# Order edges for side work: squares, row scalings and their transfers behind the weight split of their k-step

## The chip, the cores and the metric

The kernel runs on one core of one Trainium2 chip. The metric is the device time of one execution in microseconds. A core has five engines with a queue of their own each: PE (matmul), DVE (vector), ACT (scalar), POOL (GpSimd) and SP, which in this kernel issues nearly all transfers. Each queue is worked off in order. Which instruction stands where in a queue is settled at compile time, by a scheduler that goes by the order in the program, by what it takes to be ready, and by order edges that the program adds.

## The reference

One layer of a hybrid encoder, applied to two groups of requests with shared weights, 1024 and 256 tokens wide (10 blocks of 128 tokens), and to 2 x 256 rows of memory. The kernel works the 10 blocks in two groups of 5 (640 rows each). Cut to what matters:

```
hn   = rms_norm(x, norm_g)                    # x: 1280 x 2048
proj = hn @ w_in                              # conv input, gates, dt, q, k, v, mq
mk, mv = split(rms_norm(mem, mem_norm_g) @ w_mem_kv)
o = concat(ssd(silu(conv(xbc)), dt) * silu(z), window_attention(q, k, v), mem_attention(mq, mk, mv))
y = x + o @ w_out
```

All is float32. rms_norm needs, for each row, the sum of its 2048 squares.

## The kernel before

**Matrix products.** Each product runs in k-steps of 128 features. In a k-step a weight tile (`wraw`) is loaded, then split into a high part `wh` (ACT, line 203) and the rest `wl` (DVE, line 204), and three matmuls use them: high by high, high by low, low by high. There are two kinds of block:
- `block_tok` (line 231): 5 token blocks (4 for the memory), 512 or 288 columns, 16 k-steps, matmuls in lines 256 to 258. The last two k-steps are worked together.
- `block_pair` (line 1116): a scheme with 7 in place of 8 products, 8 k-steps a unit, each with 21 matmuls of 320 columns (lines 1141 to 1143). POOL forms sums of the weights (`weight_sums`, line 1096, four instructions in line 1113), and these are split too (`sh`, `sl`, by the same lines 203 and 204). It yields after every k-step but k = 6, so 7 times a unit.

**The order of the work.** First the memory's two blocks and q (group 0); then `pairs_in(0)`, ten units; then the token blocks kv and mq of group 0; then `pairs_in(1)`, ten units for group 1; then token blocks with the two "lanes" beside them (attention, state space, memory attention: generators that `pump` moves on by rates); then the output blocks. In this profile the first pair stage runs from 166 to 426.6 us, the second from 525.6 to 772.8 us.

**Side work.** Beside a pair stage a generator `side` is moved on by one step at chosen k-steps (lines 1507 and 1508).
- `first_side` (line 1351), beside the first pair stage: the squares of x's row blocks 5 to 9, by `stats` (line 1319). A row block is 4 pieces of 128 x 512, each loaded into a tile `sst` (line 1341) and squared with a sum on ACT (line 1332); after the fourth come a sum on DVE (line 1335) and `rsqrt` on POOL (lines 121 and 122) into `rx`. `x_rows(1)` then spreads `rx` over the partitions by matmuls into `prx` (line 1407), copied to `rbc` (line 1408). Then 16 rows `xrow` of 128 x 640 are loaded (line 1358), scaled on DVE (line 1172) and stored to `xs_d` (line 1364), from where the second group's rows are loaded in the kv and mq blocks (line 1166).
- `next_side` (line 1367), beside the second pair stage: the squares of the memory's 4 row blocks, in the same way. Their `rx` is used much later, in the lanes.
- `sst` and `xrow` share one buffer (`tag="sq"`).
- `keep_x` (line 1411) stores the split x to memory, 16 transfers of 640 KB, called in every k-step from the second unit on.

**Order edges.** `wsplit` leaves its two instructions in `marks`. A block `with tc.issue_after(ins)` puts what it traces on the engine of `ins` behind `ins` in that engine's queue; it makes no engine wait for another. Before the change, the lanes' steps (line 142), the planned steps (lines 1227 and 1247) and the scaling of a row (line 1360) are put behind `marks`. The squares and the loads of rows are not; the squares' loads are put behind the last `fill_direct` load (line 1340).

Of the kernel before, what the change touches and what calls it, by code (L numbers as in the profile page):

```python
# [10 lines left out]
F32 = mybir.dt.float32  # L11
# [8 lines left out]
P = 128  # L20
D = 2048
# [20 lines left out]
def hymba_encoder_kernel(  # L42
# [77 lines left out]
    def rsqrt(dst, src, scale, n):  # L120
        G.tensor_scalar(out=dst, in0=src, scalar1=scale, scalar2=EPS, op0=ALU.mult, op1=ALU.add)
        G.tensor_tensor(out=dst, in0=dst, in1=mhalf[:, :n], op=ALU.pow)
# [59 lines left out]
    def fill_direct(q, j, src, gain=None, n=640, norm=False):  # L182
# [15 lines left out]
            V.scalar_tensor_tensor(out=l, in0=ch, scalar=gain, in1=h.bitcast(F32), op0=ALU.mult, op1=ALU.subtract)  # L198
        yield

    def wsplit(raw, h, l):

        a = A.activation(h, raw, AF.Copy)  # L203
        b = V.tensor_sub(l, raw, h.bitcast(F32))  # L204
        marks[:] = a.ins, b.ins
# [12 lines left out]
    def w_in_rows(name):  # L218
        return w_laid(laid_in(name), W_AT[name][1])
# [4 lines left out]
    def w_out_rows(c):  # L224
        return w_laid(w_out_laid[c], 512)
# [5 lines left out]
    def block_tok(w, nt, evac, before_last=None, feats=range(KT), places=range(KT)):  # L231

        load, n = w
        last = len(feats) - 1
        ps = [acc.tile([P, 512], F32, tag="acc", name="acc") for _ in range(nt)]
        hls = {}
        for k in range(last + 1):
            raw = wp.tile([P, 512], F32, tag="wraw", name="wraw", bufs=RB)
            load(feats[k], raw[:, :n])
            with tc.high_priority(offset=HP[2]):  # L240
                h = wp.tile([P, 512], F32R, tag="wh", name="wh", bufs=WB)
                l = wp.tile([P, 512], F32R, tag="wl", name="wl", bufs=WB)
                wsplit(raw[:, :n], h[:, :n], l[:, :n])
            hls[k] = h, l
            if k == last - 1:
                continue
            if k == last and before_last is not None:
                before_last(k)

            for t in range(nt):  # L250
                for k_ in ((k - 1, k) if k == last else (k,)):
                    q, m = divmod(places[k_], 4)
                    h, l = hls[k_]
                    sh = cur["H", q][:, m, t * P:(t + 1) * P]
                    sl = cur["L", q][:, m, t * P:(t + 1) * P]
                    T.matmul(ps[t][:, :n], sh, h[:, :n], start=(k_ == 0), stop=False)  # L256
                    T.matmul(ps[t][:, :n], sh, l[:, :n], start=False, stop=False)  # L257
# [910 lines left out]
    def x_row(grp, r):  # L1168
        return x_turned[grp, r * P:(r + 1) * P, :]

    def scale_row(r, x):
        V.scalar_tensor_tensor(out=x, in0=x, scalar=vec[:, R_G + r:R_G + r + 1], in1=rbc, op0=ALU.mult, op1=ALU.mult)

    def p_rows(k, tiles, new=True):

# [143 lines left out]
    def stats(tiles, place, ahead=4, group=None):  # L1319

        n = 4 * len(tiles)
        group = group or n
        pieces, s4 = {}, None
        for g in range(0, n, group):
            m = min(group, n - g)
            for i in range(m + ahead):
                if i >= ahead:
                    t, c = divmod(g + i - ahead, 4)
                    if c == 0:
                        s4 = sm.tile([P, 4], F32, tag="s4", name="xs4", bufs=4)  # L1330
                    x = pieces.pop(g + i - ahead)
                    A.activation(x, x, AF.Square, accum_out=s4[:, c:c + 1])
# [15 lines left out]
    def square_place(_):  # L1348
        return fin.tile([P, 640], F32, tag="sq", name="sst")[:, :512]

    def first_side():

        yield from stats([(xrow(t), t) for t in range(5, 10)], square_place, ahead=1)
        for _ in x_rows(1):
            yield
        for r in range(KT):
            x = fin.tile([P, 640], F32, tag="sq", name="xrow")
            S.dma_start(x, x_row(1, r))
            yield
            with ExitStack() as st:  # L1360
                for ins in marks:
                    st.enter_context(tc.issue_after(ins))
                scale_row(r, x)
                S.dma_start(xs_d[r], x)
            yield

    def next_side():
        yield from stats([(mrow(i), 10 + i) for i in range(4)], square_place, ahead=1)

    def run(gen, rates, after=None, hold=0, lag=2, extra=None):  # L1370

        for k in gen:
            if after is not None and k % 4 == 3:
                pend.extend(after(k // 4))
            if hold > 0:
                for _ in range(2 if k < KT - 4 else 0):
                    if pend:
                        u = pend.popleft()()
                        next(u)
                        next(u)  # L1380
# [12 lines left out]
            if extra is not None:  # L1393
                extra(k)
# [108 lines left out]
    def pairs_in(grp, extra, side):  # L1503
        nonlocal owe
        for u, unit in enumerate(units):
            for k in block_pair(w_in_pairs, u, rows_in, ev_seven(*unit, grp), lead=2):
                if grp == 0 and (u > 3 or k not in (3, 7)) or grp and k in (0, 2, 4):
                    next(side, None)

                owe = owe + (1.4 if k < 7 else 0.0) if left else 0.0  # L1510
                while owe >= 1:
                    owe -= 1
                    if left:
                        some_left()
                if u == 0:
                    extra(32 + k)
                elif grp == 0 and keep:
                    keep_x(*keep.pop(0))

    side = first_side()  # L1520
    pairs_in(0, p_step, side)
    assert next(side, None) is None

    def left_and(f):
        def g(k):
# [7 lines left out]
        extra=left_and(lambda k: t_step(16 + k)))  # L1533
    side = next_side()
    pairs_in(1, t_step, side)
    assert next(side, None) is None
    early.close()


# [22 lines left out]
    dtb, aneg = lconst([P, 32], "dtb"), lconst([P, 32], "aneg")  # L1562

    def tok(name, i, evac, after=None, extra=None, hold=0):
        run(block_tok(w_in_rows(name), 5, evac), RATES[name], after, extra=extra, hold=hold)

    queue(1, vectors, [0])
    queue(1, dt_prep, [0])
# [53 lines left out]
    halves = [range(8), range(8, KT)]  # L1622
    for c, part_ in ((0, 0), (1, 0), (0, 1), (1, 1)):
        h = halves[part_]
        run(block_tok(w_out_rows(c), 5, ev_out(c, part_), feats=h, places=h), RATES["o" if part_ else "oa"], hold=-1,
            extra=late_rows(c, part_))
    for c in (2, 3):
        j0 = 16 * c - 48
        for k in block_tok(w_out_rows(c), 5, ev_out(c), before_last=lambda _: beside_step(j0 + 14)):
# [90 lines left out]
```

## Time and profile before

| what | value |
|---|---|
| median of 3 runs | 1840.42 us (1840.4 to 1844.22) |
| the profiled execution's own time | 1843.13 us |
| its span, first to last instruction | 1841.4 us |
| mean granted clock of TensorE | 0.992 |
| DMA | 334.20 MB, 181 GB/s over the span |

A row of a group gives line, engine, operation, tiles (out<-in), shapes and count, then busy us and the mean ns of one, then the idle time of the engine just before these instructions and what ended most of it. A row of the timeline gives start, duration, engine, line, operation and tiles, and in brackets the idle time before it and its releaser. A row of the waits gives who waited for whom, the total in us, how often, and the longest. Line numbers are those of the kernel before. PE's busy share counts overlapping matmuls once; a matmul of 320 columns can show 0.3 us and yet start every 0.15 us.

### The profile page before, as it was taken

The numbers are of one execution on the slowest core, as the hardware profiler recorded it, in microseconds if no ns is written. First come the engines' busy times: TensorE is split into PE (matmuls) and PEld (weight loads), VectorE is DVE, ScalarE is ACT, GpSimd is POOL, SyncE is SP. The second block draws the span as 40 slices with busy tenths as digits, with TensorE's granted clock in tenths as the row PEclk, the third lists the DMA queues.
The fourth block names the chain that finished last, engine by engine and source line by source line (L and its number), as shares of the span: only waits on it lengthen the run. The fifth ranks groups of instructions, "written<-read, shape, count | busy, mean of one in ns | idle before, by whom it ended". The sixth has DMA issues, their size and how long they took to land.

```text
span 1841.4 us, 31026 instructions
## 1 busy us (share of the span) xinstructions
PE 1787.4 (97%) x10306; PEld 1577.7 (86%) x10306; DVE 1327.5 (72%) x2473; ACT 951.4 (52%) x2081; POOL 676.7 (37%) x1092
## 2 busy tenths in 40 slices
PE   9999999998999999999999999999999999999999
PEld 7777999988889999988777877888777787889999
DVE  4495788895767889787677767667797765766665
ACT  6554444344554444366567447657546744443332
POOL 0104788871057889511001011000111101047775
PEclk9999999999999999999999999999999999999999
DMA  8687335555753333374545567657698765644442
GB/s 285 208 301 275 121 108 183 179 176 168 257 166 108 116 115 102 102 218 140 164 139 154 171 219 257 211 177 225 210 283 242 252 201 158 208 152 147 144 133 86
DMA packets 216177, 334.20 MB, mean 181 GB/s; under 512 B 22160, under 2 KB 84944, under 8 KB 216016
## 3 DMA queue, kind: packets, MB, share of 16 engines
q1 hardware_dynamic: 215872, 332.16, 58.0%
q8 instruction: 81, 1.33, 0.3%
q14 instruction: 80, 0.66, 0.1%
q10 hardware_dynamic: 144, 0.06, 0.0%
HBM read 255.53 MB, written 76.61 MB: 180 GB/s over the span
## 4 chain that ended last, share of the span: by engine, by line
PE 67%; DMA 13%; DVE 8%; issue 4%; ACT 3%; POOL 3%; SPq 1%; ACTq 0%; DVEq 0%; POOLq 0%
PE acc L257 8%; PE acc L258 8%; PE acc L256 8%; PE acc L1143 8%; PE acc L1141 8%; PE acc L1142 8%; PE accm L1141 3%; PE accm L1142 3%; PE accm L1143 3%; DVE wl L204 2%; PE py L873 2%; DMA sst<-in_x_sample_dram 1%; POOL ws L1113 1%; DMA wraw<-in_w_in_pairs_dram 1%; DMA rf<-ac 1%
## 5 line engine op out<-in xcount | busy, mean ns | idle before, releaser
L256 PE MATMUL acc<-wh,xH 128*128 128x512 f32 (+1 forms) x1248 | 486.9, 390 | 9.4 <-ACT wh L203 7.6
L257 PE MATMUL acc<-wl,xH 128*128 128x512 f32 (+1 forms) x1248 | 481.8, 386 | 8.0 <-DVE wl L204 7.5
L258 PE MATMUL acc<-wh,xL 128*128 128x512 f32 (+1 forms) x1248 | 478.4, 383 | 0.0
L204 DVE TENSOR_TENSOR wl<-wraw,wh 128x512 fp32r<-128x512 f32 (+1 forms) x480 | 349.5, 731 | 162.9 <-ACT wh L203 160.1
L203 ACT ACTIVATE wh<-wraw 128x512 fp32r<-128x512 f32 (+1 forms) x480 | 290.4, 612 | 186.6 <-PE acc L258 103.7
L256 PEld LDWEIGHTS acc<-wh,xH 128*128 128x128 f32 x1248 | 237.7, 191 | 56.1 <-ACT wh L203 11.5
L257 PEld LDWEIGHTS acc<-wl,xH 128*128 128x128 f32 x1248 | 237.6, 190 | 55.9 <-DVE wl L204 15.1
L203 ACT ACTIVATE sh<-ws 128x384 fp32r<-128x384 f32 x224 | 115.8, 524 | 321.4 <-POOL ws L1113 148.9
L258 PEld LDWEIGHTS acc<-wh,xL 128*128 128x128 f32 x1248 | 237.6, 190 | 42.1 <-issue 0.7
L204 DVE TENSOR_TENSOR sl<-ws,sh 128x384 fp32r<-128x384 f32 x224 | 155.8, 698 | 126.4 <-ACT sh L203 125.9
L1113 POOL TENSOR_TENSOR ws<-wraw 128x128 f32<-128x128 f32 x224 | 148.3, 662 | 261.6 <-DMA wraw<-in_w_in_pairs_dram 111.5
L1113 POOL TENSOR_TENSOR ws<-wraw,ws 128x128 f32<-128x128 f32 x224 | 154.9, 691 | 17.5
L1113 POOL TENSOR_TENSOR ws<-ws,wraw 128x128 f32<-128x128 f32 x224 | 148.7, 664 | 0.0
L1113 POOL TENSOR_TENSOR wraw<-wraw 128x128 f32<-128x128 f32 x224 | 138.6, 619 | 17.6
L581 POOL COPY lg<-nsink 128x2 f32<-128x2 f32 x40 | 16.1, 405 | 269.9 <-PE ppt L609 146.9
L1143 PE MATMUL acc<-xH,wl 128*128 128x320 f32 x320 | 99.6, 311 | 4.9 <-DVE wl L204 4.9
L1141 PE MATMUL acc<-tH,sh 128*128 128x320 f32 x320 | 100.1, 313 | 0.0
L1141 PE MATMUL acc<-xH,wh 128*128 128x320 f32 x320 | 99.1, 310 | 0.7 <-ACT wh L203 0.6
L1143 PE MATMUL acc<-tH,sl 128*128 128x320 f32 x320 | 99.5, 311 | 0.0
L1141 PE MATMUL accm<-tH,wh 128*128 128x320 f32 x320 | 98.9, 309 | 0.2
L1142 PE MATMUL acc<-xL,wh 128*128 128x320 f32 x320 | 98.9, 309 | 0.0
L1142 PE MATMUL acc<-tL,sh 128*128 128x320 f32 x320 | 98.7, 308 | 0.0
(472 smaller groups left out, 3921.6 us busy)
## 6 DMA issues: line engine op xcount, KB each, us to landing
wraw<-in_w_in_pairs_dram SPq DMA_DIRECT2D x160, 256.0 KB, 2.7
wraw<-in_w_in_laid_dram SPq DMA_DIRECT2D x128, 256.0 KB, 3.6
wraw<-in_w_out_laid_dram SPq DMA_DIRECT2D x64, 256.0 KB, 3.4
wraw<-in_w_out_pairs_dram SPq DMA_DIRECT2D x64, 256.0 KB, 2.8
xH<-xH SPq DMA_DIRECT2D x16, 640.0 KB, 5.9
xL<-xL SPq DMA_DIRECT2D x16, 640.0 KB, 6.3
rf<-ac SPq DMA_DIRECT2D x40, 256.0 KB, 4.0
rb<-ac SPq DMA_DIRECT2D x40, 256.0 KB, 4.4
```

Of the source, the lines that this page charges most:

```text
L203: a = A.activation(h, raw, AF.Copy)
L204: b = V.tensor_sub(l, raw, h.bitcast(F32))
L256: T.matmul(ps[t][:, :n], sh, h[:, :n], start=(k_ == 0), stop=False)
L257: T.matmul(ps[t][:, :n], sh, l[:, :n], start=False, stop=False)
L258: T.matmul(ps[t][:, :n], sl, h[:, :n], start=False, stop=(k_ == last))
L581: G.tensor_copy(lg[:, :, nk:nk + 1], ns8[:, rr, :].unsqueeze(2))
L873: T.matmul(py[:, h * 64:h * 64 + 64], mt[:, (h % 4) * P:(h % 4 + 1) * P], xsT[g][:, h * 64:h * 64 + 64], start=True, stop=True)
L1113: G.tensor_tensor(out=o, in0=x, in1=y, op=op)
L1141: T.matmul(ps[p], h, xh, start=(k_ == 0), stop=False)
L1142: T.matmul(ps[p], h, xl, start=False, stop=False)
L1143: T.matmul(ps[p], l, xh, start=False, stop=(k_ == 7))
```

## The change

- `behind()` is a block that enters `issue_after` for each of the marks. `side_work(tasks)` runs a list of tasks (load, f), two loads ahead: in step i it first calls f of task i - 2 and then the load of task i, all in a `behind()` block.
- The squares become tasks: 7 pieces of 320 columns a row block (the last of 128), two buffers of 320 columns in place of one of 640, 35 tasks beside the first pair stage and 28 beside the second. Their loads are no longer put behind the last `fill_direct` load.
- The scalings become 32 tasks of half a row.
- Side steps beside the first pair stage: 8 a unit (none at k = 7, two at k = 1 and 4), where it was 5 in the first four units and 7 after. Beside the second: 5 a unit (k = 0, 1, 2, 4, 5), where it was 3.
- `keep_x` runs in a `behind()` block, and only at k = 1, 3, 5.
- In `block_tok`, `middle` keeps a matmul of each k-step (the last product of the middle token block, of the second and fourth for the last two k-steps); with `spaced`, which the blocks beside the lanes pass, the split of a k-step is traced in an `issue_after` block of the matmul of two k-steps before.

```diff
+    def behind():
+        st = ExitStack()
+        for ins in marks:
+            st.enter_context(tc.issue_after(ins))
+        return st
+
+    count, middle = [0], {}
...
-                wsplit(raw[:, :n], h[:, :n], l[:, :n])
+                with tc.issue_after(middle[count[0] - 2]) if spaced and count[0] - 2 in middle else ExitStack():
+                    wsplit(raw[:, :n], h[:, :n], l[:, :n])
+            count[0] += 1
...
-                    T.matmul(ps[t][:, :n], sl, h[:, :n], start=False, stop=(k_ == last))
+                    mm = T.matmul(ps[t][:, :n], sl, h[:, :n], start=False, stop=(k_ == last))
+                if k < last and t == nt // 2:
+                    middle[count[0] - 1] = mm.ins
+                elif k == last and t in (1, 3):
+                    middle[count[0] - 2 + t // 2] = mm.ins
...
+    def side_work(tasks):
+
+        places = deque()
+        for task in tasks + [None] * 2:
+            with behind():
+                if len(places) == 2 or task is None:
+                    f, x = places.popleft()
+                    if f is not None:
+                        f(x)
+                if task is not None:
+                    load, f = task
+                    places.append((f, load()))
+            yield
+
+    def square_tasks(tiles):
+
+        out, cols = [], [(320 * i, min(320, D - 320 * i)) for i in range(7)]
+        for src, place in tiles:
+            s7 = []
+            for i, (o, n) in enumerate(cols):
+                def load(src=src, o=o, n=n):
+                    x = fin.tile([P, 320], F32, tag="sq", name="sst", bufs=2)
+                    S.dma_start(x[:, :n], src[:, o:o + n])
+                    return x
+
+                def square(x, i=i, n=n, s7=s7, place=place):
+                    if i == 0:
+                        s7.append(sm.tile([P, 7], F32, tag="s7", name="xs7", bufs=1))
+                    A.activation(x[:, :n], x[:, :n], AF.Square, accum_out=s7[0][:, i:i + 1])
+                    if i == 6:
+                        r = rx[:, place:place + 1]
+                        V.reduce_sum(out=r, in_=s7[0], axis=AX.X)
+                        rsqrt(r, r, 1.0 / D, 1)
+                out.append((load, square))
+        return out
+
+    def row_tasks():
+
+        out = []
+        for r in range(KT):
+            for c in (slice(0, 320), slice(320, 640)):
+                def load(r=r, c=c):
+                    x = fin.tile([P, 320], F32, tag="sq", name="xrow", bufs=2)
+                    S.dma_start(x, x_row(1, r)[:, c])
+                    return x
+
+                def scale(x, r=r, c=c):
+                    scale_row(r, x, c)
+                    S.dma_start(xs_d[r][:, c], x)
+                out.append((load, scale))
+        return out
...
     def keep_x(q, i, j):
-        S.dma_start(xhl_d[q][i][:, j:j + 2, :], cur["HL"[i], q].bitcast(F32)[:, j:j + 2, :])
+        with behind():
+            S.dma_start(xhl_d[q][i][:, j:j + 2, :], cur["HL"[i], q].bitcast(F32)[:, j:j + 2, :])
...
-                if grp == 0 and (u > 3 or k not in (3, 7)) or grp and k in (0, 2, 4):
+                for _ in range((0 if k == 7 else 2 if k in (1, 4) else 1) if grp == 0 else k in (0, 1, 2, 4, 5)):
                     next(side, None)
```

More of the change, by code (lines that the diff above doesn't have):

```diff
@@ L1169, in x_row, with scale_row @@
         return x_turned[grp, r * P:(r + 1) * P, :]
-    def scale_row(r, x):
-        V.scalar_tensor_tensor(out=x, in0=x, scalar=vec[:, R_G + r:R_G + r + 1], in1=rbc, op0=ALU.mult, op1=ALU.mult)
+    def scale_row(r, x, c=slice(0, 640)):
+        V.scalar_tensor_tensor(out=x, in0=x, scalar=vec[:, R_G + r:R_G + r + 1], in1=rbc[:, c], op0=ALU.mult, op1=ALU.mult)
     def p_rows(k, tiles, new=True):
@@ L1351, in first_side @@
     def first_side():
-        yield from stats([(xrow(t), t) for t in range(5, 10)], square_place, ahead=1)
+        yield from side_work(square_tasks([(xrow(t), t) for t in range(5, 10)]))
         for _ in x_rows(1):
             yield
[L1356 to L1365, printed above, removed]
+        yield from side_work(row_tasks())
@@ L1367, in next_side @@
     def next_side():
-        yield from stats([(mrow(i), 10 + i) for i in range(4)], square_place, ahead=1)
+        yield from side_work(square_tasks([(mrow(i), 10 + i) for i in range(4)]))
     def run(gen, rates, after=None, hold=0, lag=2, extra=None):
@@ L1516, in pairs_in @@
                     extra(32 + k)
-                elif grp == 0 and keep:
+                elif grp == 0 and keep and k in (1, 3, 5):
                     keep_x(*keep.pop(0))
@@ L1521, in hymba_encoder_kernel @@
     pairs_in(0, p_step, side)
-    assert next(side, None) is None
+    assert next(side, 0) == 0
     def left_and(f):
@@ L1535, in hymba_encoder_kernel @@
     pairs_in(1, t_step, side)
-    assert next(side, None) is None
+    assert next(side, 0) == 0
     early.close()
@@ L1564, in tok @@
     def tok(name, i, evac, after=None, extra=None, hold=0):
-        run(block_tok(w_in_rows(name), 5, evac), RATES[name], after, extra=extra, hold=hold)
+        run(block_tok(w_in_rows(name), 5, evac, spaced=True), RATES[name], after, extra=extra, hold=hold)
     queue(1, vectors, [0])
@@ L1624, in hymba_encoder_kernel @@
         h = halves[part_]
-        run(block_tok(w_out_rows(c), 5, ev_out(c, part_), feats=h, places=h), RATES["o" if part_ else "oa"], hold=-1,
+        run(block_tok(w_out_rows(c), 5, ev_out(c, part_), feats=h, places=h, spaced=True), RATES["o" if part_ else "oa"], hold=-1,
             extra=late_rows(c, part_))
```

6 lines of the change are left out of this document (2 added, 4 removed).

## The prediction

> **What bounds the kernel now.** The page comes first: its busy line, then the shares of the chain that ended last.
>
> ```profile
> span 1841.4 us, 31026 instructions
> ...
> PE 1787.4 (97%) x10306; PEld 1577.7 (86%) x10306; DVE 1327.5 (72%) x2473; ACT 951.4 (52%) x2081; POOL 676.7 (37%) x1092
> ...
> PE 67%; DMA 13%; DVE 8%; issue 4%; ACT 3%; POOL 3%; SPq 1%; ACTq 0%; DVEq 0%; POOLq 0%
> ```
>
> TensorE (PE) is the bound. It is idle for 1841.4 - 1787.4 = 54.0 us, and a change that takes no matmul away can win that idle time, time at a reduced clock, and little else. The next view cuts the span at the boundaries of the stages: memory blocks and q; first pair stage; kv and mq; second pair stage; all blocks beside the lanes. Columns: stretch and length; busy us and instructions of PE, PEld, DVE, ACT, POOL; granted clock; DMA share; GB/s.
>
> ```profile
> 0.00:166.00 166.00, 155.47 (x644) 122.24 (x645) 97.21 (x163) 91.27 (x182) 21.38 (x46) 0.98 0.80 267
> 166.00:426.60 260.60, 252.68 (x1690) 248.60 (x1690) 208.96 (x311) 117.17 (x219) 205.16 (x302) 0.99 0.51 160
> 426.60:525.60 99.00, 91.95 (x483) 80.11 (x482) 69.81 (x126) 51.22 (x100) 17.57 (x30) 0.97 0.74 233
> 525.60:772.80 247.20, 246.40 (x1681) 245.91 (x1680) 199.50 (x319) 112.77 (x199) 196.86 (x297) 1.00 0.36 108
> 772.80:1640.40 867.60, 843.54 (x4471) 683.86 (x4470) 622.55 (x1355) 503.65 (x1249) 95.28 (x178) 0.99 0.65 197
> ```
>
> Both pair stages issue the same matmuls. The second takes 247.2 us with PE idle for 0.8; the first takes 260.6, so 13.4 us lie there. The kv and mq stretch is idle for 99.00 - 91.95 = 7.05 us. Then the clock: the same view over four short stretches.
>
> ```profile
> 155.80:162.60 6.80, 5.85 (x14) 4.08 (x13) 2.52 (x5) 1.72 (x4) 2.74 (x7) 0.50 0.83 260
> 394.70:398.10 3.40, 3.40 (x15) 3.40 (x14) 2.54 (x4) 0.00 (x0) 1.89 (x3) 0.50 0.80 191
> 432.30:435.70 3.40, 3.40 (x14) 3.40 (x15) 3.17 (x6) 0.62 (x3) 0.00 (x0) 0.50 0.86 238
> 466.40:469.80 3.40, 3.40 (x16) 3.40 (x15) 3.40 (x7) 2.41 (x5) 0.00 (x0) 0.50 0.82 261
> ```
>
> Half a clock costs half the stretch: 3.4 us in the first, 1.7 in each other. What PE waited for stands in the waits of PE: three rows of 400 to 526 us, three of 84 to 166, one of 190 to 400.
>
> ```profile
> PE acc L256 <- ACT wh L203: 4.8, 2, 2.9
> PE acc L257 <- DVE wl L204: 1.8, 3, 0.8
> PE acc L1141 <- ACT wh L203: 0.6, 1, 0.6
> ...
> PE acc L257 <- DVE wl L204: 3.3, 6, 1.1
> PE acc L256 <- ACT wh L203: 2.7, 2, 1.4
> PE acc L256 <- ACT mvo L358: 1.5, 1, 1.5
> ...
> PE acc L1143 <- DVE wl L204: 4.7, 4, 2.9
> ```
>
> Why the split was late is read on ACT's timeline, from 426 us, 463 us and 94 us.
>
> ```profile
> 426.46 0.63 ACT L1332 ACTIVATE sst<-sst 128x512 f32<-128x512 f32 x1 [2.57 <-DMA sst<-in_mem_sample_dram]
> ...
> 430.65 0.63 ACT L1332 ACTIVATE sst<-sst 128x512 f32<-128x512 f32 x1 [3.46 <-DMA sst<-in_mem_sample_dram]
> 431.18 0.19 ACT L1332 ACTIVATION_READ_ACCUMULATOR sst<-sst 128x1 f32 x1
> 431.27 1.09 ACT L203 ACTIVATE wh<-wraw 128x288 fp32r<-128x288 f32 x3
> ...
> 463.57 0.63 ACT L1332 ACTIVATE sst<-sst 128x512 f32<-128x512 f32 x1 [2.27 <-DMA sst<-in_mem_prompt_dram]
> ...
> 95.18 0.63 ACT L1332 ACTIVATE sst<-sst 128x512 f32<-128x512 f32 x1 [1.86 <-DMA sst<-in_x_sample_dram]
> ```
>
> A square stands in ACT's queue ahead of three splits and waits 3.46 us for its transfer; the splits follow at once, and PE's longest wait of that stretch, 2.9 us, ends there. The squares of the whole kernel, by tile:
>
> ```profile
> L1332 ACT ACTIVATE sst<-sst x36: 613/632/636, 67.6 to 489.7; 128x512 f32<-128x512 f32 x36
> ...
>   ACT sst L1332: 53.6, 27
> ```
>
> The last row counts 27 of 36 squares that waited for their load, 53.6 us together. In the code they belong to the pair stages (166 to 427 us and 526 to 773 us), yet they ran from 67.6 to 489.7 us: without an order edge they went as soon as their one buffer was free, beside token blocks whose splits have no time to lose.
>
> **The change part by part.** An order edge ties an instruction to an earlier one of the same engine's queue. The marks are on ACT and DVE, so inside `behind()` the squares (ACT), sums and scalings (DVE) get edges. Transfers go out on SP and the rsqrt runs on POOL: neither gets one. The splits held back beside the lanes are on ACT and DVE, but name a matmul: I read no edge there either and take that part, and keep_x's block, at 0.
>
> *Squares leave kv and mq.* The two waits on wh (4.8 us) go, both stretches of half clock (2 x 1.7 = 3.4) with them, and 0.3 of the 1.8 us on wl, since DVE still waits there for the rows it sums: -8.5. The 0.6 us on L1141 goes too. Bounds: 0, if the clock and another late split take their place, and -(7.05 + 3.4 + 0.6) = -11.
>
> *Squares leave the first stage.* Its waits are 3.3 + 2.7 + 1.5 = 7.5 us, plus 3.4 of clock. The square at 95.18 is behind about 1.5 of it and shares in the wait on mvo. The worst group, near 153 us, has another cause on ACT's timeline:
>
> ```profile
> 152.75 0.52 ACT L203 ACTIVATE sh<-ws 128x384 fp32r<-128x384 f32 x1 [4.73 <-POOL ws L1113]
> ```
>
> That split of sums stood ahead of q's last splits and waited for POOL, at a DMA share of 0.83. Twenty square loads less make this rarer, but no edge forbids it. I take -5 of the possible -10.9; the other bound is 0.
>
> The Trainium skill bears on the clock ("TensorE: Matmul & The Clock Gate", HAM oscillation): only PE gaps over about 3.4 us bring the half clock back. Here a longest wait of 2.9 us came just before 0.50, so the trace doesn't bear the threshold out. By the rule 3.4 + 3.4 us of clock would not hang on these waits, and the sum would be 6.8 us smaller; that is the second rival.
>
> *Row scalings.* Sixteen rows become 32 half rows, in two buffers, with 8 side calls in a unit in place of 7. By tile, in the DMA issues and in SP's waits from 280 to 400 us:
>
> ```profile
> L1172 DVE SCALAR_TENSOR_TENSOR xrow<-xrow,vec,rbc x16: 869/1020/1090, 281.4 to 399.0; 128x640 f32<-128x640 f32 x16
> ...
>   DMA xrow<-in_x_turned_dram: 8.1, 6
> ...
> xrow<-in_x_turned_dram SPq DMA_DIRECT2D x16, 320.0 KB, 3.0
> ...
> xs<-xrow SPq DMA_DIRECT2D x16, 320.0 KB, 2.2
> ...
> out_dram<-yr SPq DMA_DIRECT2D x8, 320.0 KB, 2.2
> out_dram<-yr SPq DMA_DIRECT2D x16, 160.0 KB, 2.8
> ...
> SPq L1358 <- DMA xs<-xrow: 11.6, 11, 2.4
> ```
>
> A buffer's round before: load 3.0, scaling 1.0, store 2.2, two issues of some 0.33, together 6.9 us, against two calls of 24.7 / 7, or 7.1 us. After: load 2.8 (between 2.2 and 3.0; the 160 KB row is the nearest), scaling 0.5 (half; no row shows it, bounds 0.45 and 1.0), store 2.5, issues 0.7, together 6.5, against 2 x 24.7 / 8 = 6.2. Six of sixteen scalings waited before, 8.1 us in all, and the wait at 393.80 (2.9 us, clock 1.7) follows one. The new round is no looser, so I take 0; bounds -6.4 (the 4.7 us on L1143 and the clock) and +14, below. SP now issues a store and then a load that needs it landed: it has 11.6 us of such waits already, with the weight load next in its queue.
>
> The Trainium skill ("DMA: Bandwidth & Descriptors", Anatomy of one DMA, for transfers over GpSimd) gives a transfer about 2.0 us plus its bytes at 436 GB/s: an estimate of 2.4 us for 160 KB, a round of 6.0, inside 6.2, and -6.4 for this term. The 160 KB row says 2.8, and the measurement decides.
>
> *Squares enter the pair stages.* 63 squares of 320 columns replace 36 of 512. ACT copies that size in 437 ns:
>
> ```profile
> L1280 ACT ACTIVATE yu<-acc 128x320 f32<-128x320 f32 x10 | 4.4, 437 | 3.5 <-PE acc L1143 3.5
> L203 ACT ACTIVATE sh<-ws 128x384 fp32r<-128x384 f32 x77 | 39.9, 524 | 99.6 <-PE acc L1142 61.1 <-POOL ws L1113 35.8 <-PE acc L1143 2.6
> L122 POOL TENSOR_TENSOR rx<-rx,mhalf x14: 550/800/1105, 36.0 to 492.2; 128x1 f32<-128x1 f32 x14
> ```
>
> So 63 x (0.44 + 0.19) = 39 us on ACT over two stages in which it is idle for 278. In the second stage it spends 61.1 us waiting for PE to free a buffer: it runs ahead, and a square of 0.63 us behind the split is covered. Without that cover all 39 us would be PE's. Nine rsqrt of about 1 us go into POOL's queue between the weight sums; POOL is busy 205 of 260 and 197 of 247 us, and a sum it delays holds sh on ACT, then wl on DVE, then PE. A load waits on SP for the square that frees its slot, and the next weight load waits behind it. The first group's last rsqrt also comes just ahead of the matmuls that spread rx, which PE can't pass. I take +3 for all this (bounds 0 and +12: nine rsqrt that each hold PE 1.3 us). At the start two half loads may go out early: two issues of 0.33 us on SP, taken as 0.
>
> **Sum.** -8.5 - 0.6 - 5 + 0 + 3 = -11. Against the profiled execution, 1843.1 us (span 1841.4), that is 1832; the median shown is 2.7 us lower, so **1829**.
>
> **Rivals.**
> *The half rows become the wait (slower).* Over 280 to 400 us, in the first pair stage:
>
> ```profile
> 280.00:400.00 120.00, 113.70 (x745) 110.64 (x746) 103.41 (x147) 48.62 (x88) 101.30 (x144) 0.99 0.56 181
> ```
>
> DVE is idle for 16.6 us, 8.1 of them the waits above. If 32 half rows each waited what those six did (8.1 / 6 = 1.35 us), that is 43 us, 26 more than the idle time: with -14 of the rest of the sum and its +3, 1840 + 26 - 11 = 1855. It decides from about 0.9 us each: 28 us is the 16.6 us of idle time and the 11 us of gain. For it: the round is 6.5 us against 6.2, and edges force the order. Against it: two slots, and a load issued two calls ahead. If only the shortfall counts, 32 x (6.5 - 6.2) / 2 = 5 us fall inside DVE's idle time; at a round of 7.1 they are +14. Chance 0.15.
>
> *Part of the gain isn't there.* The half clock stays where it was (-11 + 6.8 = -4), or squares and rsqrt cost 8 in the pair stages in place of 3 (-6): 1834 to 1836. Chance 0.13.
>
> *Nothing to be measured.* The waits move: what kv, mq and the start lose, the pair stages give back (-14 + 12, the bound above, is -2): 1838. Chance 0.11.
>
> *The held-back splits do act.* PE is idle for 24.1 us beside the lanes; half of it gone would give 1829 - 12 = 1817, but a split made late would cost as much. Against it: no instruction in that block is on the matmul's engine. Chance 0.04 for a gain, 0.02 for a loss, which counts as slower.
>
> **How the numbers follow.** The forecast, 1815 to 1834, has 0.55. Faster by over 0.2% (3.7 us, about what a measurement of this kernel tells from no change): 0.55 + 0.13 + 0.04 = 0.72. Within: 0.11. Slower: 0.17. The range 1815 to 1841 leaves out the slower cases and few others: its low end is -11 - 10.9 - 6.4 + 3 = -25 from the median.
>
> **What would show it.** Squares between 166 and 290 and between 526 and 700 us, none beside kv or mq. kv and mq at some 89 us in place of 99, with no clock of 0.50. First stage some 161 us. The second pair stage at 247 to 250; if it passes 255, POOL or SP took the gain. In the first pair stage, idle time of DVE before xrow over 28 us would make the slower rival right. The lanes' stretch should keep its 868 us within a few us; if it doesn't, the held-back part acts after all, or the order there changed.

## The result and the profile after

The changed kernel took 1832.45 us (median of 6 runs, 1826.16 to 1836.09) beside 1841.62 us of the kernel before on the same chip: ratio 0.9948, 95% interval 0.9925 to 0.9970. It is faster by 9.2 us; the forecast was 11 us less, 1829. In a second series (first experiment below) it took 1829.78 beside 1841.24, ratio 0.9927 (0.9911 to 0.9942), 11.5 us less. The profiled execution took 1830.21 us.

The busy line and the shares of the chain that ended last, after:

```profile
span 1828.5 us, 31223 instructions
...
PE 1780.6 (97%) x10306; PEld 1573.9 (86%) x10306; DVE 1332.2 (73%) x2489; ACT 952.7 (52%) x2135; POOL 682.1 (37%) x1092
...
PE 64%; DMA 12%; issue 7%; DVE 7%; POOL 6%; ACT 3%; SPq 1%; POOLq 0%; DVEq 0%; ACTq 0%
```

PE is idle for 1828.5 - 1780.6 = 47.9 us, 6.1 less than before; its busy time fell by 6.8 us with the same 10306 matmuls: over the span, time at half a clock cost 15.4 us before and 8.6 after. The view cut at the boundaries of the stages shows where that happened. The columns are those of before: stretch and length; busy us (and instructions) of PE, PEld, DVE, ACT, POOL; clock; DMA share; GB/s. The last row, the output's pairs, was 201.0 us before.

```profile
0.00:157.40 157.40, 151.81 (x644) 122.07 (x645) 96.48 (x160) 83.89 (x156) 19.42 (x40) 0.99 0.79 269
157.40:425.70 268.30, 255.16 (x1691) 250.26 (x1691) 212.71 (x330) 124.02 (x265) 205.38 (x306) 0.99 0.54 160
425.70:515.10 89.40, 87.90 (x482) 76.32 (x481) 69.23 (x122) 44.98 (x80) 15.68 (x24) 1.00 0.73 227
515.10:762.50 247.40, 246.77 (x1682) 246.42 (x1681) 201.40 (x324) 121.51 (x253) 202.36 (x305) 1.00 0.41 123
762.50:1627.00 864.50, 841.42 (x4470) 681.81 (x4469) 622.52 (x1353) 503.20 (x1249) 97.55 (x178) 1.00 0.64 198
1627.00:1828.50 201.50, 197.54 (x1345) 197.01 (x1343) 129.82 (x203) 75.13 (x136) 141.70 (x240) 1.00 0.44 135
```

Read it row against row: the memory and q lost 8.6 us (166.0 to 157.4), kv and mq lost 9.6 (99.0 to 89.4), the first pair stage **gave back** 7.7 (260.6 to 268.3), the second 0.2, and the lanes lost 3.1. ACT's instruction counts tell why: 182 to 156 in the first row, 100 to 80 in the third; all but a few squares have left. Before, 15 of 36 squares ran in the first stretch and 10 in kv and mq; now 2 of 63 do (at 114.8 and 146.1 us) and 1 (at 505.0 us). The squares themselves, by tile:

```profile
L1390 ACT ACTIVATE sst<-sst x63: 292/455/473, 114.8 to 649.2; 128x320 f32<-128x320 f32 x54, 128x128 f32<-128x128 f32 x9
...
  DMA sst<-in_x_sample_dram: 3.0, 3
  DMA sst<-in_x_prompt_dram: 1.1, 1
...
  ACT sst L1390: 4.1, 4
```

Four of 63 waited for their load, 4.1 us in all, where 27 of 36 had waited 53.6 us. What PE still waits for in kv and mq (425.7 to 515.1 us), and then in the first pair stage from 190 us on:

```profile
PE acc L267 <- DVE wl L212: 0.9, 3, 0.4
PE acc L266 <- ACT kvraw L298: 0.6, 2, 0.4
```

```profile
PE acc L1157 <- DVE wl L212: 7.7, 6, 2.5
PE prx L1461 <- DVE rbc L1462: 3.4, 1, 3.4
```

The wait for wh, 4.8 us before, is gone from kv and mq. In the pair stage PE waits 7.7 us for splits of weights, 4.9 before. And a wait has appeared that before had at 1.5 us and for another engine: PE, about to spread `rx` into `prx` for the second time, waits 3.4 us until DVE has copied the first `prx` away (lines 1461 and 1462 were 1407 and 1408). The same place before:

```profile
PE prx L1407 <- POOL ws L1113: 1.5, 1, 1.5
```

The clock after, over the four stretches in which it was halved (a fifth begins 0.1 us before the end):

```profile
149.00:152.40 3.40, 3.38 (x7) 2.33 (x8) 2.06 (x4) 0.59 (x1) 0.21 (x1) 0.50 0.58 208
282.10:288.90 6.80, 6.02 (x23) 6.05 (x24) 2.48 (x7) 0.52 (x1) 3.42 (x8) 0.50 0.14 41
1398.30:1401.70 3.40, 3.40 (x11) 2.73 (x10) 3.36 (x6) 2.15 (x4) 0.00 (x0) 0.50 1.02 325
1514.30:1517.70 3.40, 3.33 (x11) 2.78 (x12) 1.47 (x3) 1.23 (x2) 1.22 (x2) 0.51 0.42 128
```

None lies in kv and mq now. One of double length (it costs some 3.4 us) goes with the wait for `prx`. Why that copy was late is on DVE's timeline:

```profile
279.51 0.77 DVE L212 TENSOR_TENSOR sl<-ws,sh 128x384 fp32r<-128x384 f32 x1 [0.91 <-ACT sh L211]
280.21 1.07 DVE L324 SCALAR_TENSOR_TENSOR c<-u,vec,c 128x638 f32<-128x638 f32 x1
281.20 0.94 DVE L212 TENSOR_TENSOR wl<-wraw,wh 128x512 fp32r<-128x512 f32 x1
282.06 0.68 DVE L1462 COPY rbc<-prx 128x512 f32<-128x512 f32 x1
```

PE had nothing to do after 279.20 + 0.31 = 279.5 us. DVE still had a split of sums, a step of the convolution and a split of weights ahead of the copy. The second copy of this spread, at 283.69 us, then waited for PE in its turn.

### The profile page after: what moved, and what is told of

It is laid out like the page before. It is cut to its first block, busy times and chain, and to the rows that moved or that the text cites. A ratio compares the mean times of both kernels' runs of the same rounds, so it can differ in the third digit from the quotient of the medians.

```text
span 1828.5 us, 31223 instructions
## 1 busy us (share of the span) xinstructions
PE 1780.6 (97%) x10306; PEld 1573.9 (86%) x10306; DVE 1332.2 (73%) x2489; ACT 952.7 (52%) x2135; POOL 682.1 (37%) x1092
## 4 chain that ended last, share of the span: by engine, by line
PE 64%; DMA 12%; issue 7%; DVE 7%; POOL 6%; ACT 3%; SPq 1%; POOLq 0%; DVEq 0%; ACTq 0%
PE acc L266 8%; PE acc L267 8%; PE acc L268 7%; PE acc L1157 7%; PE acc L1155 7%; PE acc L1156 7%; POOL ws L1127 3%; PE accm L1155 3%; PE accm L1156 3%; PE accm L1157 3%; PE py L887 2%; DMA wraw<-in_w_in_pairs_dram 1%; DVE wl L212 1%; POOL wraw L1127 1%; PE pmo L733 1%
## 5 line engine op out<-in xcount | busy, mean ns | idle before, releaser
L212 DVE TENSOR_TENSOR wl<-wraw,wh 128x512 fp32r<-128x512 f32 (+1 forms) x480 | 350.9, 734 | 152.2 <-ACT wh L211 149.0
L1127 POOL TENSOR_TENSOR ws<-wraw 128x128 f32<-128x128 f32 x224 | 152.5, 681 | 337.2 <-DMA wraw<-in_w_in_pairs_dram 194.0
L1127 POOL TENSOR_TENSOR ws<-wraw,ws 128x128 f32<-128x128 f32 x224 | 150.3, 671 | 17.6
```

Source lines behind the costliest of these rows:

```text
L1127: G.tensor_tensor(out=o, in0=x, in1=y, op=op)
```

## The experiments

The theory after the result: the **edge on the squares** brings the whole gain, in two stages; the pair stage gives part back through the wait at the second spread of `rx`; the half rows, the two buffers and the other two parts are worth nothing. The rivals: the squares need the second buffer too; the half rows cost or win something; `keep_x` or the lanes' splits have a share.

Lengths of the stages in us, one profile each, cut at the first matmul of the next stage's kind. "Spread later" means two more side steps between the two spreads of `rx`.

| kernel | memory, q | pairs 1 | kv, mq | pairs 2 | lanes, output blocks | median time |
|---|---|---|---|---|---|---|
| before | 166.0 | 260.6 | 99.0 | 247.2 | 867.6 | 1839 to 1842 |
| changed | 157.4 | 268.3 | 89.4 | 247.4 | 864.5 | 1832.45 |
| changed, again | 155.6 | 265.7 | 89.8 | 247.6 | 868.6 | 1829.78 |
| before + edge | 158.6 | 261.3 | 90.1 | 247.5 | 867.8 | 1828.11 |
| changed, no edge | 164.0 | 263.1 | 95.6 | 247.2 | 867.6 | 1843.76 |
| before + half rows | 165.3 | 269.3 | 89.5 | 246.9 | 865.9 | 1844.78 |
| changed, whole rows | 156.8 | 264.9 | 91.2 | 247.7 | 864.1 | 1828.18 |
| changed + spread later | 158.4 | 260.7 | 88.9 | 247.7 | 866.4 | 1823.58 |
| changed, whole rows + spread later | 158.1 | 259.9 | 89.4 | 247.4 | 869.2 | 1826.10 |
| before + edge + spread later | 159.1 | 260.2 | 91.3 | 247.6 | 871.0 | 1823.82 |
| changed + stores behind loads | 156.5 | 268.4 | 91.5 | 247.3 | 869.1 | 1832.22 |
| before + edge + spread later + stores behind loads | 152.4 | 266.2 | 89.4 | 247.0 | 865.7 | 1830.30 |
| changed + real hold | 152.7 | 263.3 | 88.0 | 246.5 | 862.2 | 1826.31 |
| before + edge + spread later + real hold | 157.5 | 259.0 | 90.4 | 246.6 | 860.4 | 1822.36 |

**The changed kernel again.** No edit.

> The changed kernel once more, nothing edited, for a second profile of it. If single profiles of the first stage and of the first pair stage differ by some 5 us from run to run (the kernel with real holds, whose program is the changed one's up to the lanes, differed by 4.7 and 5.0 us there), this profile has the first stage within 152 to 158 us, the pair stage within 263 to 269 us, and the stage of the key/values and memory queries again within 88 to 91.5 us, with a median time of 1828 to 1834 us. Rival: the two stages are steady (157.4 and 268.3 us again within 1 us), and the difference came from something else.

The first two stages came out at 155.6 and 265.7 us, 1.8 and 2.6 less; the real hold's profile, the same program up to the lanes, had 152.7 and 263.3. So these two stages differ by up to 5 us between single profiles, and the lanes by 4 (864.5 and 868.6). A row of the table is to be read with that in mind: differences of the groups below, not of single rows, carry the conclusions. The half clock is part of it. In the first stage it was on for 3.4 us in both profiles of the changed kernel and not at all in the real hold's; beside the lanes for 6.8 and 13.7 us. A profiled execution can also lie off the median of its kernel: those of no edge, half rows, the real hold (1815.61 us) and edge, later spread and stores behind loads (1823.34) were the shortest of their runs, and that of edge and later spread (1831.82) the longest. The wait at the spread repeated to the hundredth, 3.38 us, but the half clock with it was half as long, 3.4 us:

```profile
PE acc L1157 <- DVE wl L212: 7.3, 4, 2.4
PE prx L1461 <- DVE rbc L1462: 3.4, 1, 3.4
```

**The edge alone**, in the kernel before: 512 columns, one buffer, the old steps.

```diff
-                    A.activation(x, x, AF.Square, accum_out=s4[:, c:c + 1])
+                    with ExitStack() as st:
+                        for ins in marks:
+                            st.enter_context(tc.issue_after(ins))
+                        A.activation(x, x, AF.Square, accum_out=s4[:, c:c + 1])
```

> The kernel before with one thing more: each square is put behind the weight split of its k-step (512 columns, one buffer, old calls). Theory (a square that stands ahead of a split and waits for its load is what cost): the squares leave the first stage and the kv and mq stretch, which take 157 to 159 and 89 to 91 us as after the change (before 166.0 and 99.0), the second pair stage stays under 250, and the whole is 1824 to 1830 us. Rival (two buffers and loads two tasks ahead are what helped): with one buffer the squares still wait for their loads, now in the pair stages; first and second pair stage grow by 5 us or more each, and the whole is within 4 us of before.

1828.11 us (4 runs, 1826.44 to 1828.98), ratio 0.9926 (0.9911 to 0.9942). The 36 squares, by tile:

```profile
L1335 ACT ACTIVATE sst<-sst x36: 615/617/637, 114.9 to 634.8; 128x512 f32<-128x512 f32 x36
...
  ACT sst L1335: 8.9, 8
```

They ran to 634.8 us in place of 489.7 and waited 8.9 us in place of 53.6. Memory and q took 158.6 us, kv and mq 90.1. Everything that the change wins is here, without its other parts. The rival that a second buffer is needed falls.

**The changed kernel without the edge:** all else as in the change. The same block also held the sums and the scalings of the rows, and these lose their edges too; the scalings run from 285.6 to 403.8 us, in neither of the two stages that matter here.

```diff
-            with behind():
+            with ExitStack():
```

> The changed kernel without the edges in the side tasks (320 columns, two buffers, two tasks ahead stay). Theory: the squares run early again, some beside kv and mq and in the first stage; kv and mq take 95 to 99 us, the first stage 161 to 166, the whole 1838 to 1848 us. Rival: the two buffers alone keep the waits short: kv and mq at 89 to 91 us, the whole within 4 us of the changed kernel, 1832.

1843.76 us (10 runs), ratio 1.0019 (1.0002 to 1.0036). The squares' tile:

```profile
L1390 ACT ACTIVATE sst<-sst x63: 297/472/477, 46.8 to 463.1; 128x320 f32<-128x320 f32 x54, 128x128 f32<-128x128 f32 x9
...
  ACT sst L1390: 45.8, 40
```

They run early again and wait 45.8 us, although there are two buffers and fewer bytes in each piece. Memory and q are back at 164.0 us, kv and mq at 95.6, with PE waiting there for the splits again:

```profile
PE acc L266 <- ACT wh L211: 2.7, 4, 1.4
```

No half clock came with these shorter waits, and kv and mq stayed below the 99.0 us of before. The edge alone added the edge and this one took it away, and both moved the same two stages: that the edge is the cause is shown, not argued.

**Half rows alone**, in the kernel before, in the halves of its one buffer, with 8 steps a unit.

```diff
...
+                if len(held) == 2 or i >= 2 * KT:
+                    r, c, x = held.popleft()
+                    V.scalar_tensor_tensor(out=x, in0=x, scalar=vec[:, R_G + r:R_G + r + 1], in1=rbc[:, c], op0=ALU.mult, op1=ALU.mult)
+                    S.dma_start(xs_d[r][:, c], x)
+                if i < 2 * KT:
+                    r, c = i // 2, slice(320 * (i % 2), 320 * (i % 2) + 320)
+                    x = sq[:, c]
+                    S.dma_start(x, x_row(1, r)[:, c])
+                    held.append((r, c, x))
...
```

> The kernel before with the row scalings alone as 32 half rows in two halves of the one buffer, 8 side calls a unit in the first pair stage. Theory (in the first pair stage, which grew by 7.6 us, some 5 are the wait for the second spread of rx and 2 the half rows): the first pair stage takes 261 to 264 us (before 260.7), the rest as before, the whole 1840 to 1845 us. Rival (the round of a half row is the wait): 266 us or more, DVE idle before the scalings over 15 us, the whole 1846 us or more.

1844.78 us (10 runs), ratio 1.0013 (1.0002 to 1.0025). The pair stage grew to 269.3 us and kv and mq shrank to 89.5. The time is the theory's, but its 261 to 264 us for the stage was missed, and the rival's 266 or more was met. Two things are mixed in it. The rows were done by 356 us, which freed the buffer, so the memory's squares, unedged here, ran from 365 to 427 us inside the pair stage, not beside kv and mq: this part shows the squares' cost moving with the squares. But most of what PE lost in the stage lies earlier, while the half rows were scaled (244 to 356 us): 7.6 us of waits for splits and two half clocks, at 319.3 and 346.6 us. So this run doesn't clear half rows, at least in the halves of one buffer. The scalings read from 280 to 400 us, 22 of the 32 (busy us, mean ns, then DVE's idle time before them):

```profile
L1365 DVE SCALAR_TENSOR_TENSOR sq<-sq,vec,rbc 128x320 f32<-128x320 f32 x22 | 14.6, 664 | 6.6 <-DMA sq<-in_x_turned_dram 6.6
```

**Whole rows again**, in the changed kernel: 16 rows of 640 columns in one buffer; the squares keep their two halves of it.

```diff
...
-        yield from side_work(row_tasks())
+        for r in range(KT):
+            x = sq
+            S.dma_start(sq, x_row(1, r))
+            yield
+            with behind():
+                scale_row(r, x)
+                S.dma_start(xs_d[r], x)
+            yield
```

> The changed kernel with whole rows again (one buffer, load and scaling in turns); squares as changed. Theory: the wait for the second spread of rx stays (about 3 us and 3 of half clock), the first pair stage takes 264 to 268 us, after the change 268.3; the whole 1828 to 1833. Rival (half rows cost the 7.6 us): 260 to 262 us, the whole 1822 to 1826.

1828.18 us (4 runs), ratio 0.9929 (0.9905 to 0.9953); the pair stage took 264.9 us beside 268.3 and 265.7. The wait at the spread is untouched:

```profile
PE acc L1157 <- DVE wl L212: 4.0, 4, 2.3
PE prx L1471 <- DVE rbc L1472: 3.4, 1, 3.4
```

So it isn't the rows that cause it. Whether half rows cost anything, the next two tell.

**The second spread two steps later**, in the changed kernel.

```diff
+            if grp and o == 0:
+                yield
+                yield
```

> The changed kernel with two side steps between the first and the second spread of rx, so that the copy of the first has time to leave DVE's queue before PE reaches the second. Theory (PE's 3.4 us at the second spread wait for that copy, and the half clock after it follows the wait): the wait and the 6.8 us of half clock go, the first pair stage takes 262 to 264 us (268.3 with the change), the whole 1826 to 1829. Rival (PE would have had to wait for the splits there anyway): 267 to 269 us, nothing changes.

1823.58 us (4 runs, 1820.48 to 1824.96), ratio 0.9915 (0.9895 to 0.9936). The pair stage took 260.7 us, less than the 262 to 264 that was expected, and of PE's waits in it from 190 us on these are left:

```profile
PE acc L1157 <- DVE wl L212: 6.0, 5, 2.1
PE acc L1155 <- DVE r L1303: 0.4, 1, 0.4
```

The wait at the spread is gone and so is the half clock with it; two others, of 3.4 us each, stand later in the stage (331.4 and 386.1 us). The profiles with the changed steps and edged squares fall in two groups: with the old spread 268.3, 265.7, 264.9, 268.4 and 263.3 us (mean 266.1), with the later spread 260.7 and 259.9 (mean 260.3). The wait was 3.2 to 3.4 us in all five of the first group. The half clock with it was 6.8 us long in two of them, 3.4 in two, and absent in one (the real hold's), so it cost some 2 us on average. Together that is near the difference, 5.8 us. Most of what the change gave back is this wait.

**Whole rows and the later spread together**, in the changed kernel (both diffs above).

> The changed kernel with whole rows again and the two side steps between the spreads of rx. Theory that the half rows cost something of themselves: pair stage 257 to 260 us, 2 to 4 us below the changed kernel with the two steps alone (260.7 us, 1823.6 us in all), so 1819 to 1822 us. Rival: the half rows are free once the spread waits for nothing: 1822 to 1826 us.

1826.10 us (6 runs), ratio 0.9916 (0.9895 to 0.9936). The pair stage took 259.9 us, as the theory had it, but beside half rows' 260.7 and 1823.58 us that is no gain. With the spread out of the way, half rows cost nothing that the time shows: the rival holds. A small cost isn't excluded, since PE waited less for splits in this stage with whole rows: 4.7 us beside 6.0 here, and with the old spread 4.0 beside the changed kernel's 7.7 and 7.3.

**Edge and later spread in the kernel before.**

> Before, with two edits alone: the edge behind the weight split for the squares, and the two side steps between the first and the second spread of rx; the squares, rows, scalings and stores are as before. Theory: the two gains are of different waits and add up: pair stage 256 to 261 us, key/values and memory queries 88 to 91 us, median time 1820 to 1825 us. Rival: before's pair stage (260.7 us) has no wait at the spread that costs much, so the second edit gives nothing: 1827 to 1831 us, as with the edge alone.

1823.82 us (6 runs, 1819.91 to 1831.82), ratio 0.9907 (0.9887 to 0.9926). The time is inside the theory's 1820 to 1825 us. The pair stage took 260.2 us beside 261.3 with the edge alone, although PE's wait at the spread, 2.6 us there (1.5 in the kernel before), is gone. The median is 4.3 us below the edge alone, yet the intervals of the ratios overlap, and the one profile, of the longest of the six runs, has no stage that carries it; whether the two add up stays open.

**`keep_x` behind the weight loads.** The change's block around `keep_x` is an edge to ACT's and DVE's instructions, and the store goes out on SP: with or without it the built program is the same, instruction for instruction and wait for wait. This makes the edge real, on SP.

```diff
...
-        with behind():
+        with tc.issue_after(last_w[0].ins):
```

> The changed kernel with the 16 stores of the split x put behind the newest weight load of the pair stage, which is issued by the same engine, so that the edge binds. Theory (these stores run beside q because an edge behind ACT and DVE doesn't hold SP, and they make the first pair weights late, 5.3 us to landing): they move behind 150 us, the weight sums and the split before q's end come earlier, the first stage takes 152 to 155 us (157.4 with the change), the first pair stage stays at 268. Rival (they only fill idle DMA time): the first stage stays at 157 to 158, or the first pair stage grows by as much.

1832.22 us (10 runs), ratio 0.9965 (0.9951 to 0.9979). Memory and q took 156.5 us, between the theory's 152 to 155 and the rival's 157 to 158, and the pair stage 268.4. No gain in the time: the theory that the stores delay the weight loads there isn't borne out.

**Edge, later spread and stores behind loads** in the kernel before.

> The kernel before with three things alone: the edge for each square, the second spread of rx two side steps later, and the stores of the split x behind the newest weight load. Theory: the three gains add up: first stage 152 to 156 us, first pair stage 258 to 261, kv and mq 90, the whole 1818 to 1824. Rival (the stores beside the first pair stage collide with the loads of rows, or later rows make DVE's queue fuller): the first pair stage takes 264 us or more and the whole is no better than the edge alone, 1828.

1830.30 us (6 runs), ratio 0.9947 (0.9926 to 0.9967), no better than the edge alone. Memory and q took 152.4 us, but so short a stage is no sign of the stores: the real hold's profile, with the stores where the change has them, had 152.7, and these two are the only profiles without a half clock in it. The pair stage took 266.2 us without any half clock, and PE waited for splits in it 11 times:

```profile
PE acc L1143 <- DVE wl L204: 8.5, 11, 3.0
```

**A real hold beside the lanes.** The change's `spaced` part ties splits on ACT and DVE to a matmul on PE. `issue_after` binds only instructions of that matmul's engine, so this too leaves the built program the same. This makes the order real across engines, without a wait of its own.

```diff
+                for ins in marks if spaced and count[0] - 2 in middle else ():
+                    tc.add_manual_dep(ins, middle[count[0] - 2].name, mybir.DependencyInfo(
+                        mybir.DependencyClass.NoSync, mybir.DependencyReason.DATA), reason="held")
```

> The changed kernel with an order edge that does tie each split beside the lanes to the middle matmul of two k-steps before, across engines and in issue order alone. Theory (in the changed kernel these splits are tied to nothing, so that part was worth 0): here the order beside the lanes changes, and the stretch of 864.5 us with it, by up to 12 us either way; my guess is 855 to 862 us. Rival (splits stand there already where the edge would put them): within 2 us of 864.5.

1826.31 us (7 runs, 1815.61 to 1832.35), ratio 0.9935 (0.9914 to 0.9956), an interval that overlaps the changed kernel's. The lanes and output blocks took 862.2 us in the shortest of the seven runs, at the edge of the 855 to 862 that was guessed.

**The hold on top of edge and later spread**, in the kernel before, with the same lines.

> The run before it, and beside the lanes each weight split really held until the middle matmul of the k-step two before. Theory that the hold is worth something: lanes and output 858 to 863 us (865 to 868 without), 3 to 6 us off the time of the run beside it. Rival: the hold moves a split that nothing was late for; the time is within 2 us of the run beside it.

1822.36 us (5 runs, 1816.03 to 1824.15), ratio 0.9885 (0.9866 to 0.9904), 1.5 us below the run beside it: by the time, the rival's case. The lanes' stretch disagrees, 860.4 us beside 871.0. First the row with the hold, then the one without:

```profile
753.50:1613.90 860.40, 841.69 (x4471) 682.60 (x4470) 621.87 (x1354) 500.79 (x1249) 96.37 (x178) 0.99 0.65 199
```

```profile
758.30:1629.30 871.00, 845.24 (x4470) 685.02 (x4470) 623.07 (x1354) 503.14 (x1249) 97.67 (x178) 0.99 0.64 196
```

Part of this is the clock: it was halved beside the lanes for 10.2 us with the hold and for 17.1 without. With half of such time taken off, the twelve profiles without a hold lie at 860.7 to 864.2 us, the two with one at 858.8 and 855.3. That speaks for a small gain, of a few us. But both profiles with a hold are of short runs of their kernels (the shortest of seven, the second of five), and the medians don't settle it. This is the fastest kernel tried, though its interval overlaps those of the three others with an edge and a later spread whose stores aren't tied to loads.

## Why the prediction was right, point by point

| term | predicted | profile after | second profile |
|---|---|---|---|
| kv and mq | -8.5 | -9.6 | -9.2 |
| memory and q | -5 | -8.6 | -10.4 |
| half rows, squares, rsqrt and spread in the pair stages, with the 0.6 us on L1141 | 0 + 3 - 0.6 | +7.7 and +0.2 | +5.1 and +0.4 |
| lanes and output | 0 | -3.1 + 0.5 | +1.0 + 0.1 |
| sum | -11 | -12.9 | -13.0 |

- **Squares leave kv and mq: right, also in its parts.** The waits on wh and both half clocks went. The 0.6 us on L1141, which the prediction tells here, lay before 426.6 us, in the first pair stage, and went too. One square still ran beside kv and mq, where none was expected. The clock rule that the prediction set against the trace (the Trainium skill, "TensorE: Matmul & The Clock Gate", HAM oscillation: only gaps over about 3.4 us bring the half clock) would have kept the 3.4 us of clock. The measurement decides against it: before, a longest wait of 2.9 us there came with two half clocks; in the eleven profiles with the edge the longest wait there is 0.4 to 1.4 us, and none has a half clock. Elsewhere in the profile after, one at 149.0 us follows waits of 1.7 and 1.3 us, and one at 1398.3 us a wait of 2.6.
- **Squares leave the first stage: right in direction, too small.** The prediction took half of the stage's 10.9 us, because the worst group had another cause, a split of sums that waits for POOL. That cause is still there, and longer (ACT's timeline):

```profile
145.66 0.52 ACT L211 ACTIVATE sh<-ws 128x384 fp32r<-128x384 f32 x1 [7.44 <-POOL ws L1127]
```

  What PE waited for around it (84 to 166 us; the last row is already the pair stage's):

```profile
PE acc L266 <- ACT wh L211: 1.7, 1, 1.7
PE acc L267 <- DVE wl L212: 1.3, 1, 1.3
PE acc L1155 <- ACT qs L291: 1.3, 2, 1.0
```

  So PE lost only two waits to it, 1.7 and 1.3 us, and 1.7 us of clock. Over the whole stage PE lost 10.5 us of idle time and 3.4 of clock before, and 5.6 and 1.7 after. With the squares out of ACT's queue and 4 square loads issued in the stage in place of 16, the same cause costs less. The two can't be told apart by these runs: the edge removes both.
- **The pair stages: the step that was too small.** The prediction gave +3 for squares, rsqrt, loads on SP and the spread together, and named the spread: "The first group's last rsqrt also comes just ahead of the matmuls that spread rx, which PE can't pass." The place was right and the releaser wrong. No rsqrt held PE; the second spread needs the `prx` that DVE is still to copy, and the changed steps brought it where DVE had 2.5 us of other work in front. It cost 3.4 us and in this profile a half clock of some 3.4; moving it by two steps took the wait away and 5.8 us off the stage on average. The rest was covered as said: in the changed kernel with the later spread the stage is at 259.9 to 260.7 us, and the second pair stage, with nearly all of the memory's squares in it where before had none, is at 246.5 to 247.7 in all profiles with the edge (247.2 before).
- **Row scalings at 0: right as far as the time shows.** The slower rival needed more than 28 us of DVE's idle time before `xrow`; this is what there was:

```profile
L1186 DVE SCALAR_TENSOR_TENSOR xrow<-xrow,vec,rbc x32: 535/600/765, 292.7 to 405.3; 128x320 f32<-128x320 f32 x32
...
  DMA xrow<-in_x_turned_dram: 6.4, 8
  issue: 2.4, 1
```

  Eight scalings of 32 waited 6.4 us, about as long as six of 16 before (8.1). The scaling was mis-sized, 0.60 us for the 0.5 taken, inside the bounds; the load landed in 2.7 us for the 2.8 taken and the store in 2.5 as taken (medians).
- **Held-back splits and `keep_x` at 0: right.** Both edges bind nothing, as was read from the engines of the marks. The lanes' -3.1 us in the first profile became +1.0 in the second. Here too it is the clock: half a clock cost 6.8 us beside the lanes before, 3.4 in the first profile after and 6.8 in the second.
- **The sum was right partly by luck.** The first stage gave 4 to 5 us more than was forecast, and the pair stages took 3 to 6 more. In the first profile the lanes added 3.1, from a clock that no part of the change reaches.

What stays open: why the half clock comes in some profiles of a stage and not in others (with the edge on the squares it cost the first stage 0, 1.7 or 3.4 us, which is a good part of its spread of 152.4 to 159.1), whether a real hold beside the lanes wins its few us, whether half rows cost a little, and whether the later spread wins anything in the kernel before.

## What to carry to other kernels

Side work that "belongs" to a stage in the code runs wherever the scheduler finds its buffer free; look at first and last start of its tile in the profile, and tie it with an order edge on the engine whose queue it would block. Such an edge can cost more elsewhere than it seems, through a change of step that moves one awkward instruction: look for a wait that grew in the stage that took the work in, and move that instruction alone. An edge that names an instruction of another engine may bind nothing, so compare the programs before a gain is put down to it.

## What the runs showed of the hardware

- The half clock came back after short waits: after 1.7 and 1.3 us within 2 us of each other (149.0 us), and after 2.6 us (1398.3 us). In all profiles it stayed for 3.4 us or 6.8, but for stretches that run past the end of the program. The wait of 2.6 us thus cost some 4.3. It didn't come after every such wait: in the same profile one of 2.5 us, at 365 us, brought none, and at the spread, in the same program so far, waits of 3.2 to 3.4 us brought 6.8 us of it, 3.4 or none.
- Half the columns didn't take half the time on DVE: 128 x 320 took 600 ns (median) where 128 x 640 had taken 1020, so 32 half rows kept DVE busy for 20.4 us, 16 rows for 15.8.
- Half the bytes hardly shortened a transfer: a half row of 160 KB took 2.7 us to load and 2.5 to store, a row of 320 KB 3.0 and 2.2 (medians, from issue to landing).
